# Feature-major products: three 256-column matmuls per k-tile into one range of PSUM, two feature blocks a bank

## The chip, the cores and the metric

The kernel runs on one core of one Trainium2 chip. The metric is the device time of one execution in microseconds; the median of several executions is compared. A core has a TensorE (PE, with its weight loads shown as PEld), a VectorE (DVE), a ScalarE (ACT), a GpSimd (POOL) and a SyncE (SP, which issues the DMAs here).

## What is computed

One decoder layer on 256 tokens of 2048 features, all in float32. Cut to what matters here:

```python
h = rms_norm(x, g_mix)
proj = h @ w_in                      # split into qkv_a, z_a, b_a, a_a, q_b, k_b, v_b, f_b, q_m, gates
qkv_a = causal_conv_silu(qkv_a, conv_w)     # 4 taps along the tokens, 3072 features
q_a, k_a, v_a = split(qkv_a)                # l2-normed, then the gated delta rule, 8 heads
...                                         # forgetting attention, memory attention, gated sum, w_out
x = x + y @ w_out
h2 = rms_norm(x, g_mlp)
x = x + square(relu(h2 @ w_ff1)) @ w_ff2    # 8192 hidden features

def causal_conv_silu(x, w):
    xp = pad(x, k_w - 1 zeros ahead of the first token)
    y = xp[:, 0:s] * w[0]
    for i in range(1, k_w):
        y = y + xp[:, i:i + s] * w[i]
    return silu(y)
```

## The kernel before

Every float32 product is made of three products of rounded parts: a matrix is split into a high part (rounded to the type fp32r) and a low part (the rest), and high x high, high x low and low x high are summed in PSUM. Weights come from HBM in chunks of 1 MB (`weights`, L155); each chunk is split in two halves by `split_half` (L146): an ACT copy rounds (L151), a DVE subtraction gives the rest (L152). Both are issued with a raised priority, so they run ahead of the products. There are 5 buffers for halves of either kind and 4 for chunks. Activations are split once, when they are made.

There are two kinds of product. `gemm_a` (L162) is token-major: an activation block of 128 x 128 is the stationary operand, a slice of 512 weight columns moves, and each k-tile (128 of the features that are summed over) has three matmuls of 512 columns for each of the two blocks of 128 tokens (L176 to L178). `gemm_b` (L191) is feature-major: a weight block of 128 x 128 is stationary and the 256 tokens move. It is called for pairs of feature blocks, 128 features each, with 16 k-tiles. It makes the q, k and v of the delta rule (`gdn_gemm`, L508, 24 blocks in 12 pairs) and the hidden layer of the squared-relu mlp (L925 on, 64 blocks in 32 pairs). Its activations stand as `Pairs` (L82): for each k-tile the 256 high and the 256 low columns are neighbours, so that `both(k)` is one operand of 512 columns. A k-tile then has two matmuls, both at L203: the high weights with the 512 columns into a whole bank of PSUM, and the low weights with the 256 high columns into its first half. In the last k-tile the two are issued in the opposite order. When a block is done, ACT copies the second half of the bank to SBUF (L205) and DVE adds the first half to it (L206) and writes the block's result to SBUF. For the convolution this result lies in a padded tile `xp` of 260 columns a block, whose first 4 are set to zero; ACT scales it by the first tap, DVE adds the other three (L500, L502). For the mlp ACT applies Relu (L931), DVE squares (L932), and `split` (L329) makes high and low parts.

The order of the work on each engine is the order of the program, raised priorities aside. Around the products run chains (the decay terms, the delta rule, attention) written as generators: `spawn` (L127) adds one, and `tick` (L131), called after each block and each chunk, runs one stage of every chain. `conv_pair` (L495) is such a chain: taps, then Silu and squares, then 8 one-column matmuls that sum the squares (L528), or transposes for v. PSUM is used as two pools of 4 banks, `pacc` for the products (tag `acc`) and one for all else (`sm`). One product stands apart: `head_scalars` (L402) has the three products of 256 columns each (L187 to L189, in `mm3`) with 96 weight columns.

Of the kernel before, what the change touches and what calls it, by code (L numbers as in the profile page):

```python
# [24 lines left out]
# columns of the packed vectors  # L25
# [3 lines left out]
# columns of the shape-only constants  # L29
# [10 lines left out]
def body(ctx: ExitStack, tc: tile.TileContext, I, out, dbg=None):  # L40
# [23 lines left out]
    class Blocks:  # L64
        """n blocks [128, 256], four to a tile"""
# [16 lines left out]
    class Pairs:  # L82
        """n blocks [hi 256 | lo 256], two to a tile"""
# [7 lines left out]

        def both(self, k):
            return self.t[k // 2][:, k % 2].rearrange("p a t -> p (a t)")
# [14 lines left out]
    # ---------------------------------------------------------------- constants  # L108
# [15 lines left out]
    # ---------------------------------------------------------------- interleaving  # L124
# [6 lines left out]
    def tick():  # L131
        """one more stage of each running chain"""
        for g in list(bg):
            if next(g, 0) == 0:
                bg.remove(g)
# [6 lines left out]
    # ---------------------------------------------------------------- weights  # L142
# [12 lines left out]
    def weights(src, ahead=PRI):  # L155
        """hi/lo of one chunk, in two halves"""
        with tc.high_priority(ahead):
            w = wtile(src.shape[1])
            nc.sync.dma_start(w, src)
            return [split_half(w, i) for i in range(2)]  # L160

    def gemm_a(srcs, act, evac, first=None, final=False):  # L162
        """token-major [2][128, 512] for one group of 512 columns"""
        ps = [acc(), acc()]
        nk = len(srcs) * 4
        for c, src in enumerate(srcs):
            parts = weights(src) if first is None else first[c]
            order = [(k4, tb) for k4 in range(4) for tb in range(2)]
            if final and c == len(srcs) - 1:
                order.sort(key=lambda o: o[1])  # L170
            for k4, tb in order:
                k = c * 4 + k4
                xh, xl = act(k)
                wh, wl = (t[:, k4 % 2 * 512:k4 % 2 * 512 + 512] for t in parts[k4 // 2])
                t = slice(tb * 128, tb * 128 + 128)
                mm(ps[tb], xh[:, t], wh, start=(k == 0), stop=False)  # L176
                mm(ps[tb], xh[:, t], wl, start=False, stop=False)  # L177
                mm(ps[tb], xl[:, t], wh, start=False, stop=(k == nk - 1))  # L178
                if final and k == nk - 1:
                    evac(tb, ps[tb])  # L180
            tick()
        for tb in range(2):
            if not final:
                evac(tb, ps[tb])
# [6 lines left out]
    def gemm_b(srcs, act, dst):  # L191
        """feature-major: chunks of [16 kt, 128 features], each into a [128, 256] of dst"""
        t = t2("lo")
        for f, src in enumerate(srcs):
            ps = acc()
            parts = weights(src)
            for k in range(KT):
                wh, wl = (t_[:, k % 8 * 128:k % 8 * 128 + 128] for t_ in parts[k // 8])
                ops = [(ps, wh, act.both(k)), (ps[:, 0:256], wl, act(k)[0])]
                if k == KT - 1:  # L200
                    ops.reverse()
                for i, (o, w, x) in enumerate(ops):
                    mm(o, w, x, start=(k == 0 and i == 0), stop=(k == KT - 1 and i == 1))  # L203
            tick()
            A.copy(t[:, f, :], ps[:, 256:512])  # L205
            V.tensor_tensor(dst[:, f, :], ps[:, 0:256], t[:, f, :], ALU.add)  # L206

    # ---------------------------------------------------------------- normed inputs
# [5 lines left out]
    def split_scaled(dst, xt, q, gcol, rows=None, ks=range(4)):  # L214
        """hi/lo of (transposed activations * gain [* a factor per token]) for 4 k-tiles"""
        for k in ks:
            g = pk[:, gcol + q * 4 + k:gcol + q * 4 + k + 1]
            h, l = dst(q * 4 + k)
            if rows is None:
                A.activation(h, xt[:, k, :], AF.Copy, scale=g)  # L220
                V.scalar_tensor_tensor(l, xt[:, k, :], g, h.bitcast(F32), ALU.mult, ALU.subtract)
            else:
                V.scalar_tensor_tensor(xt[:, k, :], xt[:, k, :], g, rows, ALU.mult, ALU.mult)
                A.copy(h, xt[:, k, :])
                V.tensor_tensor(l, xt[:, k, :], h.bitcast(F32), ALU.subtract)

    def row_stats(name, src):
        """1 / rms of each token"""
# [18 lines left out]
    # the first chunk and its k-tiles in halves, alternating  # L247
# [12 lines left out]
    def prep_x():  # L260
# [6 lines left out]
        # rstd of x along the free axis, on every partition  # L267
# [11 lines left out]
    # gains with the softmax scales folded in  # L279
# [4 lines left out]
    def head_scale(ps, rs, nh, dh, f2):  # L284
        """rstd of each head (times rs of the token)"""
# [15 lines left out]
    def heads_T(n, dst, tb, gains):  # L301
        """token-major [128, 512] transposed into dst[:, 0:4, tok block], gains per feature"""
# [18 lines left out]
    def query_T(ps, rs, nh, dh, dst, tb, gains, f2):  # L321
        """without the token's factor f2, which the logits get"""
        head_scale(ps, rs, nh, dh, f2)
        n = t2("hn", (P, 512))
        A.copy(n, ps)
        yield 1
        heads_T(n, dst, tb, gains)
# [5 lines left out]
    # ---------------------------------------------------------------- memory attention  # L333
# [60 lines left out]
    # ---------------------------------------------------------------- per-head scalars b, a, f  # L394
# [7 lines left out]
    def head_scalars():  # L402
# [15 lines left out]
        # log1p(e) = ln(u) + (e - (u - 1)) / u  # L418
# [5 lines left out]
        # rows 0..7: sigmoid(b) = exp(min(t, 0)) / u  # L424
        A.activation(beta, mn[0:32, :], AF.Exp)
        V.tensor_tensor(beta, beta, r_[0:32, :], ALU.mult)
        # rows 64..71: log f = min(t, 0) - log1p, and its running sum
# [3 lines left out]
        # rows 32..39: g = -exp(a_log) * softplus, running sums within chunks of 64  # L431
# [9 lines left out]
        # terms of j, per chunk of i  # L441
# [14 lines left out]
        # rows to every partition  # L456
# [3 lines left out]
        # columns: beta, cum, terms of j  # L460
# [11 lines left out]
    # E[j, i] = exp(decay from j to i), zero for j > i  # L472
# [17 lines left out]
    # ---------------------------------------------------------------- gated delta rule  # L490
# [4 lines left out]
    def conv_pair(xp, ft0, dst, then):  # L495
        """features ft0, ft0+1 of q/k/v: conv + silu -> dst [128, 2, 256]"""
        y = t2("cy")
        for f in range(2):
            cw = lambda i: pk[:, C_CONV + (ft0 + f) * 4 + i:C_CONV + (ft0 + f) * 4 + i + 1]
            A.activation(y[:, f, :], xp[:, f, 1:257], AF.Copy, scale=cw(0))  # L500
            for i in range(1, 4):
                V.scalar_tensor_tensor(y[:, f, :], xp[:, f, 1 + i:257 + i], cw(i), y[:, f, :], ALU.mult, ALU.add)  # L502
# [5 lines left out]
    def gdn_gemm(hf):  # L508
# [3 lines left out]
        # columns (k/q, token block, head): sums of squares  # L512
# [41 lines left out]
        for w, base in ((0, 8), (1, 0), (2, 16)):  # L554
            for pr_ in range(2):
                ft0 = base + hf * 4 + pr_ * 2
                xp = tp.tile([P, 2, 260], F32, tag="xp", name=nm("xp"), bufs=2)
                V.memset(xp[:, :, 0:4], 0.0)
                gemm_b([I["w_qkv"][ft0], I["w_qkv"][ft0 + 1]], hact, xp[:, :, 4:260])
# [5 lines left out]
                last = spawn(conv_pair(xp, ft0, dst, then))  # L565
# [4 lines left out]
    def gdn_chain(hf, st):  # L570
        kT, qT, vt, rq, sc = (st[n] for n in ("kT", "qT", "vt", "rq", "sc"))
        # M^T = KK * E * beta_j / |k_j|^2 ; A^T = QK * E * beta_j / |k_j|^2
        Eh = E[hf]
        # [0]: j in block 0, i in 0..255; [1]: j and i in block 1
# [15 lines left out]
        # (I + M) inverted for the 32x32 diagonal blocks, one per partition  # L590
# [5 lines left out]
        Mu = t4("Mu", (NU, 32, 32))       # [j, i]  # L596
        nc.sync.dma_start(Mu, dM.rearrange("t h (b j) i -> (t h b) j i", b=4))
        X = t4("X", (NU, 32, 32))         # [i, c]
# [40 lines left out]
        # transposed inverses of the 64x64 diagonal blocks  # L639
# [10 lines left out]
        # the solution, block by block, and the outputs  # L650
# [69 lines left out]
    # ---------------------------------------------------------------- forgetting attention  # L720
# [72 lines left out]
    # ---------------------------------------------------------------- gates and up projections  # L793
    y, yT = [], []

    def tok_tiles(name):
        """token-major [2][128, 2048] and its [128, 512] pieces"""
# [35 lines left out]
    # ---------------------------------------------------------------- the order of the parts  # L833
# [53 lines left out]
    # ---------------------------------------------------------------- output projection, residual  # L887
# [30 lines left out]
    # 1 / (mean(x^2) + eps), the square of rstd  # L918
# [6 lines left out]
    # ---------------------------------------------------------------- squared-relu mlp  # L925
    for q in range(4):
        u = Split("u", 16)
        for fp in range(8):
            r = t2("fr")
            gemm_b([I["w_ff1"][q * 16 + fp * 2 + i] for i in range(2)], h2, r)  # L930
            A.activation(r, r, AF.Relu)  # L931
            V.tensor_tensor(r, r, r, ALU.mult)  # L932
# [35 lines left out]
def prep(inp):  # L968
# [3 lines left out]
    def blk_a(w):        # [N/512, K/512, 128, 4*512]  # L972
# [4 lines left out]
    def blk_b(w):        # [N/128, 128, 16*128]  # L977
# [4 lines left out]
    def xT(x):           # [128, 16, 256]  # L982
# [52 lines left out]
```

## Time and profile before

| | |
|---|---|
| median of 3 runs | 1746.89 us (1746.37 to 1747.86) |
| span of the profiled execution | 1744.4 us |
| PE busy, matmuls | 1732.4 us, 8548 |
| PEld busy, weight loads | 1460.1 us, 8548 |
| DVE busy | 1037.3 us |
| ACT busy | 846.1 us |
| POOL busy | 40.5 us |
| read from HBM | 325.08 MB, 188 GB/s over the span |

The profile is of one execution; the median is of others, so the span stands beside it. Matmuls overlap each other: the time given for one reaches from its start to its end, and the next may start before. The distance of two starts is read from the timeline. A weight load overlaps with matmuls too.

### The profile page before, as it was taken

What the parts mean: (1) busy time and instruction counts of PE and PEld (TensorE: products, weight loads), DVE (VectorE), ACT (ScalarE), POOL (GpSimd) and SP (SyncE); (2) the same over time, 40 slices, a digit from 0 to 9 for tenths busy, and PEclk for the clock granted to TensorE, in tenths of its full rate; (3) what the DMA queues carried; (4) which work ended last, traced back from release to release, by engine and by line L of the source; (5) the groups of instructions that cost most, each with busy time, mean ns of one, the idle gap of its engine ahead of it and who ended that gap; (6) DMA issues with size and microseconds to landing.
All of it is one profiled execution on the core that took longest, in us unless ns stands there. A gap on an engine that the chain in (4) does not pass through costs nothing.

```text
span 1744.4 us, 21495 instructions
## 1 busy us (share of the span) xinstructions
PE 1732.4 (99%) x8548; PEld 1460.1 (84%) x8548; DVE 1037.3 (59%) x1379; ACT 846.1 (49%) x1144; POOL 40.5 (2%) x45
## 2 busy tenths in 40 slices
PE   8999999999999999999999999999999999999999
PEld 6888888888888888888888888888888888888887
DVE  5747777986654555555555566655665566556653
ACT  7656755435554345544444555533553355334542
POOL 0000000101000000000000000000000000000000
PEclk9999999999999999999999999999999999999999
DMA  9755444553545545455556555555555555555562
GB/s 380 286 190 173 145 166 151 174 173 132 183 142 193 193 170 204 172 193 193 190 198 233 176 190 190 181 194 192 184 193 193 193 186 177 195 196 187 193 200 90
DMA packets 53524, 329.11 MB, mean 189 GB/s; under 512 B 9888, under 2 KB 10544, under 8 KB 15664
## 3 DMA queue, kind: packets, MB, share of 16 engines
q1 hardware_dynamic: 53424, 327.74, 52.9%
q8 instruction: 67, 1.10, 0.2%
q14 instruction: 33, 0.27, 0.0%
HBM read 325.08 MB, written 2.64 MB: 188 GB/s over the span
## 4 chain that ended last, share of the span: by engine, by line
PE 99%; DVE 0%; DMA 0%; POOL 0%; ACT 0%; SPq 0%; issue 0%; DVEq 0%; POOLq 0%
PE acc L203 28%; PE acc L176 22%; PE acc L178 22%; PE acc L177 22%; PE sm L581 0%; PE sm L384 0%; PE sm L305 0%; PE sm L528 0%; PE sm L356 0%; DMA wf<-w_kv 0%; PE sm L670 0%; PE sm L664 0%; PE sm L899 0%; PE sm L785 0%; PE sm L688 0%; PE sm L675 0%
## 5 line engine op out<-in xcount | busy, mean ns | idle before, releaser
L152 DVE TENSOR_TENSOR wlo<-wf,whi 128x1024 fp32r<-128x1024 f32 x594 | 726.0, 1224 | 608.6 <-ACT whi L151 607.8
L151 ACT CAST whi<-wf 128x1024 fp32r<-128x1024 f32 x594 | 623.2, 1051 | 756.3 <-PE acc L178 556.6
L203 PE MATMUL acc<-h,whi 128*128 128x512 f32 x1408 | 496.0, 399 | 0.0
L203 PE MATMUL acc<-h,wlo 128*128 128x256 f32 x1408 | 380.8, 281 | 0.0
L203 PEld LDWEIGHTS acc<-h,whi 128*128 128x128 f32 x1408 | 260.2, 188 | 56.7
L176 PE MATMUL acc<-whi,h 128*128 128x512 f32 x704 | 278.2, 395 | 0.0
L178 PE MATMUL acc<-whi,h 128*128 128x512 f32 x704 | 274.4, 390 | 0.0
L177 PE MATMUL acc<-wlo,h 128*128 128x512 f32 x704 | 274.2, 389 | 0.0
L203 PEld LDWEIGHTS acc<-h,wlo 128*128 128x128 f32 x1408 | 265.8, 189 | 7.8
L176 PE MATMUL acc<-whi,uh 128*128 128x512 f32 x512 | 199.2, 389 | 0.0
L177 PE MATMUL acc<-wlo,uh 128*128 128x512 f32 x512 | 199.2, 389 | 0.0
L178 PE MATMUL acc<-whi,ul 128*128 128x512 f32 x512 | 199.2, 389 | 0.0
L178 PEld LDWEIGHTS acc<-whi,h 128*128 128x128 f32 x704 | 132.2, 188 | 28.1
L176 PEld LDWEIGHTS acc<-whi,h 128*128 128x128 f32 x704 | 132.2, 188 | 27.0 <-issue 0.5
L177 PEld LDWEIGHTS acc<-wlo,h 128*128 128x128 f32 x704 | 132.3, 188 | 26.4
L177 PEld LDWEIGHTS acc<-wlo,uh 128*128 128x128 f32 x512 | 96.1, 188 | 20.1
L178 PEld LDWEIGHTS acc<-whi,ul 128*128 128x128 f32 x512 | 96.1, 188 | 20.0
L176 PEld LDWEIGHTS acc<-whi,uh 128*128 128x128 f32 x512 | 96.1, 188 | 19.5
L176 PE MATMUL acc<-whi,mh 128*128 128x512 f32 x128 | 50.9, 400 | 7.4 <-ACT whi L151 7.4
L177 PE MATMUL acc<-wlo,mh 128*128 128x512 f32 x128 | 51.0, 398 | 0.0
L178 PE MATMUL acc<-whi,ml 128*128 128x512 f32 x128 | 50.8, 397 | 0.0
L176 PE MATMUL acc<-whi,yh 128*128 128x512 f32 x128 | 50.1, 392 | 0.0
(262 smaller groups left out, 1467.2 us busy)
## 6 DMA issues: line engine op xcount, KB each, us to landing
wf<-w_ff SPq DMA_DIRECT2D x128, 1024.0 KB, 4.7
wf<-w_gate SPq DMA_DIRECT2D x48, 1024.0 KB, 4.7
wf<-w_qkv SPq DMA_DIRECT2D x24, 1024.0 KB, 4.8
wf<-w_fox SPq DMA_DIRECT2D x24, 1024.0 KB, 4.8
wf<-w_up SPq DMA_DIRECT2D x24, 1024.0 KB, 4.8
wf<-w_out SPq DMA_DIRECT2D x16, 1024.0 KB, 4.8
wf<-w_kv SPq DMA_DIRECT2D x15, 1024.0 KB, 12.2
wf<-w_mq SPq DMA_DIRECT2D x8, 1024.0 KB, 4.8
```

Of the source, the lines that this page charges most:

```text
L151: A.copy(hi, c)
L152: V.tensor_tensor(lo, c, hi.bitcast(F32), ALU.subtract)
L176: mm(ps[tb], xh[:, t], wh, start=(k == 0), stop=False)
L177: mm(ps[tb], xh[:, t], wl, start=False, stop=False)
L178: mm(ps[tb], xl[:, t], wh, start=False, stop=(k == nk - 1))
L203: mm(o, w, x, start=(k == 0 and i == 0), stop=(k == KT - 1 and i == 1))
```

## The change

`gemm_b` takes one bank for a pair of feature blocks, 256 columns for each. A k-tile has three matmuls of 256 columns into the block's half: high weights with high columns, high weights with low columns, low weights with high columns. The sum of the three is formed in PSUM. Only the first matmul of a pair has the start flag and only the last the stop flag. The copy and the add behind each block are gone, and `gemm_b` returns the bank, seen as two blocks of 256. The convolution reads it directly: the last tap scales the block unshifted on ACT, and DVE adds the other three into the tokens from 1, 2 or 3 on, so that the padded tile, its zeroing and its buffers go. `gdn_gemm` runs the first stage of each convolution (the taps) at once with `next(last)`, not at the next tick. In the mlp Relu reads the bank, and the square is made by ACT in place of DVE. `both` is dropped; the layout of `Pairs` stays. Comments and docstrings are dropped as well; those lines are left out here.

```diff
@@ class Pairs
-        def both(self, k):
-            return self.t[k // 2][:, k % 2].rearrange("p a t -> p (a t)")
@@ gemm_b
-    def gemm_b(srcs, act, dst):
-        t = t2("lo")
+    def gemm_b(srcs, act):
+        ps = acc()
         for f, src in enumerate(srcs):
-            ps = acc()
+            o = ps[:, f * 256:f * 256 + 256]
             parts = weights(src)
             for k in range(KT):
                 wh, wl = (t_[:, k % 8 * 128:k % 8 * 128 + 128] for t_ in parts[k // 8])
-                ops = [(ps, wh, act.both(k)), (ps[:, 0:256], wl, act(k)[0])]
-                if k == KT - 1:
-                    ops.reverse()
-                for i, (o, w, x) in enumerate(ops):
-                    mm(o, w, x, start=(k == 0 and i == 0), stop=(k == KT - 1 and i == 1))
+                xh, xl = act(k)
+                mm(o, wh, xh, start=(f == 0 and k == 0), stop=False)
+                mm(o, wh, xl, start=False, stop=False)
+                mm(o, wl, xh, start=False, stop=(f == 1 and k == KT - 1))
             tick()
-            A.copy(t[:, f, :], ps[:, 256:512])
-            V.tensor_tensor(dst[:, f, :], ps[:, 0:256], t[:, f, :], ALU.add)
+        return ps.rearrange("p (f t) -> p f t", f=2)
@@ conv_pair
-    def conv_pair(xp, ft0, dst, then):
+    def conv_pair(ps, ft0, dst, then):
         y = t2("cy")
         for f in range(2):
             cw = lambda i: pk[:, C_CONV + (ft0 + f) * 4 + i:C_CONV + (ft0 + f) * 4 + i + 1]
-            A.activation(y[:, f, :], xp[:, f, 1:257], AF.Copy, scale=cw(0))
-            for i in range(1, 4):
-                V.scalar_tensor_tensor(y[:, f, :], xp[:, f, 1 + i:257 + i], cw(i), y[:, f, :], ALU.mult, ALU.add)
+            A.activation(y[:, f, :], ps[:, f, :], AF.Copy, scale=cw(3))
+            for i in (2, 1, 0):
+                n = 253 + i
+                V.scalar_tensor_tensor(y[:, f, 256 - n:], ps[:, f, 0:n], cw(i), y[:, f, 256 - n:], ALU.mult, ALU.add)
         yield 1
@@ gdn_gemm
-                xp = tp.tile([P, 2, 260], F32, tag="xp", name=nm("xp"), bufs=2)
-                V.memset(xp[:, :, 0:4], 0.0)
-                gemm_b([I["w_qkv"][ft0], I["w_qkv"][ft0 + 1]], hact, xp[:, :, 4:260])
+                ps = gemm_b([I["w_qkv"][ft0], I["w_qkv"][ft0 + 1]], hact)
...
-                last = spawn(conv_pair(xp, ft0, dst, then))
+                last = spawn(conv_pair(ps, ft0, dst, then))
+                next(last)
@@ squared-relu mlp
-            gemm_b([I["w_ff1"][q * 16 + fp * 2 + i] for i in range(2)], h2, r)
-            A.activation(r, r, AF.Relu)
-            V.tensor_tensor(r, r, r, ALU.mult)
+            ps = gemm_b([I["w_ff1"][q * 16 + fp * 2 + i] for i in range(2)], h2)
+            A.activation(r, ps, AF.Relu)
+            A.activation(r, r, AF.Square)
```

## Rows read from the trace of the kernel before

**Rows 1.** The page: busy time, granted clock in 40 slices, the chain by line.
```profile
PE 1732.4 (99%) x8548; PEld 1460.1 (84%) x8548; DVE 1037.3 (59%) x1379; ACT 846.1 (49%) x1144; POOL 40.5 (2%) x45
...
PEclk9999999999999999999999999999999999999999
...
PE acc L203 28%; PE acc L176 22%; PE acc L178 22%; PE acc L177 22%; PE sm L581 0%; PE sm L384 0%; PE sm L305 0%; PE sm L528 0%; PE sm L356 0%; DMA wf<-w_kv 0%; PE sm L670 0%; PE sm L664 0%; PE sm L899 0%; PE sm L785 0%; PE sm L688 0%; PE sm L675 0%
```

**Rows 2.** Waits of PE: what waited for what, us in total, times, longest.
```profile
PE acc L176 <- ACT whi L151: 7.4, 1, 7.4
PE sm L465 <- ACT Lm L365: 0.3, 1, 0.3
```

**Rows 3.** The page's groups: line, engine, operation, shapes, count | busy us, mean ns.
```profile
L203 PE MATMUL acc<-h,whi 128*128 128x512 f32 x1408 | 496.0, 399 | 0.0
L203 PE MATMUL acc<-h,wlo 128*128 128x256 f32 x1408 | 380.8, 281 | 0.0
...
L203 PEld LDWEIGHTS acc<-h,wlo 128*128 128x128 f32 x1408 | 265.8, 189 | 7.8
...
L176 PEld LDWEIGHTS acc<-whi,h 128*128 128x128 f32 x704 | 132.2, 188 | 27.0 <-issue 0.5
L177 PEld LDWEIGHTS acc<-wlo,h 128*128 128x128 f32 x704 | 132.3, 188 | 26.4
```

**Rows 4.** The chain in order of time, merged: start us, length us, what.
```profile
1207.85 90.45 PE acc L203 x512
```

**Rows 5.** Timeline of PE, end of a block: start us, length us, instruction, merged count.
```profile
1103.21 0.40 PE L203 MATMUL acc<-h,wlo 128*128 128x256 f32 x2
1103.45 0.63 PE L203 MATMUL acc<-h,whi 128*128 128x512 f32 x2
```

**Rows 6.** Timeline of PE in a stretch of `gemm_a`, 24 matmuls apart.
```profile
1300.18 0.39 PE L176 MATMUL acc<-whi,uh 128*128 128x512 f32 x1
...
1305.62 0.39 PE L176 MATMUL acc<-whi,uh 128*128 128x512 f32 x1
```

**Rows 7.** Timeline of PE in a quicker stretch of L203; first two rows 12 k-tiles apart.
```profile
292.49 0.39 PE L203 MATMUL acc<-h,whi 128*128 128x512 f32 x1
...
296.65 0.39 PE L203 MATMUL acc<-h,whi 128*128 128x512 f32 x1
...
297.23 0.40 PE L203 MATMUL acc<-h,wlo 128*128 128x256 f32 x2
297.46 0.40 PE L203 MATMUL acc<-h,whi 128*128 128x512 f32 x1
```

**Rows 8.** Timeline of PE: the first matmul of `head_scalars`, and the first after it.
```profile
144.17 0.28 PE L187 MATMUL sm<-h,whi 128*96 128x256 f32 x1
...
149.82 0.40 PE L203 MATMUL acc<-h,whi 128*128 128x512 f32 x1
```

**Rows 9.** Groups by form, 1035 to 1120 us, with idle time before and its releaser.
```profile
L152 DVE TENSOR_TENSOR wlo<-wf,whi 128x1024 fp32r<-128x1024 f32 x31 | 38.0, 1225 | 28.5 <-ACT whi L151 28.5
L151 ACT CAST whi<-wf 128x1024 fp32r<-128x1024 f32 x30 | 31.5, 1050 | 30.1 <-PE acc L203 30.1
L206 DVE TENSOR_TENSOR fr<-acc,lo 128x256 f32<-128x256 f32 x15 | 6.3, 418 | 0.0
L205 ACT COPY lo<-acc 128x256 f32<-128x256 f32 x15 | 5.4, 363 | 0.0
...
L932 DVE TENSOR_TENSOR fr<-fr 128x512 f32<-128x512 f32 x7 | 4.8, 685 | 0.0
L931 ACT ACTIVATE fr<-fr 128x512 f32<-128x512 f32 x7 | 4.4, 627 | 0.0
```

**Rows 10.** Groups by form, 150 to 316 us, the stage of q, k and v.
```profile
L502 DVE SCALAR_TENSOR_TENSOR cy<-xp,pk,cy 128x256 f32<-128x256 f32 x64 | 28.2, 482 | 2.9 <-ACT cy L500 2.7
L500 ACT ACTIVATE cy<-xp,pk 128x256 f32<-128x256 f32 x22 | 10.6, 508 | 0.8 <-DVE xp L206 0.8
...
L504 ACT ACT_TABLE_LOAD x4 | 5.1, 1283 | 0.1
```

## The prediction

> **What bounds the kernel now.** I read the page first. PE is busy for 1732.4 of 1744.4 us, and of the chain that ended last the two matmuls of `gemm_b` (L203) are 28% and the three of `gemm_a` (L176 to L178) 66% [rows 1]. A busy TensorE may still be one that is fed late, so I read the waits of PE next: two rows, 7.4 us at the very start and 0.3 us, and nothing at L203 [rows 2]. The granted clock is at the upper level, 2.4 GHz, in all 40 slices; DVE is busy for 59%, ACT for 49% [rows 1]. So the time is the number of matmuls times the spacing at which TensorE starts them, and every other engine works in its shadow. The change can move the end in one way of weight: by what one k-tile costs TensorE. The groups of L203 count 1408 k-tiles (88 blocks of 16), each with one 512-column and one 256-column matmul and a weight load for each [rows 3]. The means in these groups (399 and 281 ns) are latencies that overlap; for the cost I need start-to-start times, which the chain and the timeline give.
>
> **What a k-tile costs before.** In the squared-relu stage the chain has three runs of 90.45 us with 512 matmuls each, one of which is shown: 256 k-tiles, 353.3 ns a k-tile [rows 4]. That is 1408 x 353.3 = 497 us, the 28% of the page.
>
> **What it will cost after.** The k-tile becomes three 256-column matmuls, each with its own load of 128 weight columns. The moved columns are the same (768); a matmul and a load are added, 1408 of each. The trace has no long stream of 256-column matmuls with 128-column weights, so I bound the price from its neighbours.
>
> First, two 256-column matmuls in a row stand at the end of each block, where the last k-tile is reversed. In the steady squared-relu stage they start at 1103.21 and the 512 behind them 0.24 us later, as at the end of the next two blocks: 120 ns each [rows 5]. Second, by subtraction: the 512-column matmuls of `gemm_a` go at 24 in 5.44 us, 226.7 ns [rows 6]; in a quicker stretch of L203 twelve k-tiles take 4.16 us, 346.7 ns [rows 7]; 346.7 - 226.7 = 120 ns for the 256. Two roads give 120 ns, so three give **360 ns, 6.7 ns above the 353.3 of now**. The sum is 1408 x 6.7 ns = 9.4 us.
>
> Both ends of the unknown. Low: at the end of the quicker stretch the two in a row take only 0.23 us, 115 ns each [rows 7], so 345 ns, 1408 x -8.3 = -11.7 us. Exactly three 256-column matmuls per k-tile stand in the trace once, in `head_scalars` (L187 to L189), but with 96 weight columns: 16 k-tiles from 144.17 to 149.82, 353 ns, no difference [rows 8]. High: L203 mostly runs in the slower of two paces, 353.3 and not 346.7, 6.7 ns more over two matmuls; if each of the three pays that, 3 x (120 + 3.3) = 370 ns, +23.5 us; if the 256-column one had borne all of it, 3 x 126.7 = 380 ns, +37.5 us. I take 360: its two rows have the weight width and the moving size of the changed kernel, and `head_scalars` loads a quarter less per matmul.
>
> The Trainium skill, "TensorE: Matmul & The Clock Gate", section "Wait — 56ns, not 53.3ns?", gives a warm matmul of N columns N / 2.4 GHz and a fixed 2.5 ns or so. By it a 512 takes 215.8 ns, and the added matmul would cost 2.5 ns per k-tile, 3.5 us in all. That would put the time at 1750.4 us, the edge of no change, beside rival (a) below. The trace disagrees with the size: it shows 226.7 ns for that 512 [rows 6].
>
> **The evictions.** All of this lies beside TensorE. Removed, once in each of the 88 blocks: an ACT copy of 363 ns and a DVE add of 418 ns [rows 9], so 32 us of ACT and 37 us of DVE. Moved: 32 squares of 685 ns leave DVE (22 us) and become ACT squares; the nearest row is Relu of that shape, 627 ns, so 20 us [rows 9]. Should the square need another function table than Relu and the copies, a load of 1283 ns, as at L504 [rows 10], could come twice per pair, 2.6 us; bounds 0 and 2.6 us. Even then ACT has, per pair of blocks (32 x 353 ns = 11.3 us), 4 casts of 1050 ns, Relu, square and cast at some 0.63 us each and 2.6 us: 8.7 us. I cost it at nothing; the cover is that casts of the weights already wait for PE to free buffers, 30.1 us in 85 us [rows 9], so they run ahead. Without that cover each pair would pay its excess over 11.3 us.
>
> The convolution reads PSUM: 2 scaled copies on ACT (508 ns each now) and 6 taps on DVE (482 ns each) per pair [rows 10]. The zero padding of `xp` and its memsets go. I take the same durations; the nearest DVE row of that size that reads PSUM, the add L206, takes 418 ns with two tensor operands [rows 9], so the taps lie between 418 and 482. Its first stage moves: `next(last)` issues these 2 + 6 instructions straight behind the pair's matmuls, not after the next pair's first block, past the other chains' stages and weight splits of that block in the ACT and DVE queues; no DMA, SP or POOL instruction moves with it. Silu, the squares and their 8 small matmuls (L528) follow one tick earlier each. The wait of the first copy for the pair's last matmul holds up the ACT queue where L205 did so before, for the same matmul; the taps do it for DVE as L206 did. The small matmuls still come two blocks, 11.3 us, behind the taps, whose chain is 2 x 508 + 6 x 482 + two ACT passes of the size of Relu, 2 x 627, or 5.2 us. So nothing is late on TensorE.
>
> A bank is held by a pair until its last read, some 4 us beyond the last matmul. Before a pair took two banks of `pacc`, now one; of four, the same bank comes up three pairs later, 33.9 us. Nothing waits.
>
> **The rivals.**
> (a) *Cost goes by moved columns alone*, so that 768 columns cost the same in two matmuls or three, or nearly so. For it: `head_scalars` and L203 both take 353 ns [rows 4, 8]. Against it: L203 itself has two paces for the same columns [rows 4, 7], and `gemm_a` moves 512 columns in less than 512/768 of either [rows 6]. Time: no change, 1746.9 us.
> (b) *The slower pace for all three matmuls*, 370 ns: +23.5 us, 1770.4 us. For it: most of the L203 runs are in it [rows 4]. It decides if the stream locks into it from the first block on.
> (c) *The other side, faster*: a stream of equal matmuls runs as the pairs at 115 ns: -11.7 us, 1735.2 us. The mechanism is that in an even stream each load hides behind the matmul ahead of it without the loss that the uneven pairs show. It pays from 117.7 ns a matmul downwards. For it, the 0.23 us [rows 7]; against it, 0.24 us in the steady stage [rows 5].
> (d) *The change does not do what it says*: the same `wh` stands in two matmuls in a row, and its second load is left out; then the third matmul comes cheaper, at most back to the quick pace, 346.7 ns: -9.4 us, 1737.5 us. Against it: `gemm_a` uses `xh` twice in a row and has 704 loads for L176 and 704 for L177 [rows 3].
> (e) *TensorE waits for an eviction or a weight split* because an in-order queue is held: about 1 us at each of 44 pairs would give 44 us, 1791 us. It decides only if a pair's work on ACT or DVE passes 11.3 us; on DVE it is 4 x 1.22 + 6 x 0.48 = 7.8 us [rows 9, 10].
>
> **How the numbers follow.** The profiled execution has a span of 1744.4 us, 2.5 us under the median of 1746.89; I add the difference to the median. Forecast: 1746.9 + 9.4 = 1756.3 us (span 1753.8). Chances: forecast (356 to 364 ns) 0.46, (a) 0.24, (b) 0.18, (c) 0.07, (d) 0.02, (e) 0.03. The range takes in the forecast, (a) and (b), 0.88 of the chance, and no more of the low end than 351 ns, three times 117: 1744 to 1770.5 us. A measurement of this kernel tells some 0.2% from no change, 3.5 us or 2.5 ns a k-tile. Faster by more: (c), (d) and a little of (a), 0.10. Within: (a) and the low edge of the forecast, 0.25. Slower: the rest, 0.65.
>
> **What would show it.** The group of the `gemm_b` matmuls must have 4224 entries, all 128x256, and as many loads. Its long chain runs in the squared-relu stage should have 768 matmuls in 92.2 us for 256 k-tiles; 90.4 us speaks for (a), 94.7 us for (b), under 90 us for (c) or (d). PE's waits should stay under 10 us, L205 and L206 be gone, and DVE's busy time fall by some 60 us. I am wrong if the pace of `gemm_a` moves too, if PE waits appear at `gemm_b`, or if the stream of 256-column matmuls settles at another spacing than the two in a row did.

## The result, and the profile after

| | before | after |
|---|---|---|
| median of 4 runs each, us (range) | 1746.63 (1745.84 to 1747.86) | 1757.4 (1757.27 to 1757.6) |
| ratio to before, 95% interval | | 1.0061 (1.0047 to 1.0076) |
| span of the profiled execution, us | 1744.4 | 1755.4 |
| matmuls and weight loads, each | 8548 | 9956 |

The forecast was 1756.3 us, slower by 9.4; the kernel became slower by 10.8 us, the span by 11.0. The page after, answering to [rows 1]: busy time, the clock, the chain by line.

```profile
PE 1742.5 (99%) x9956; PEld 1535.5 (87%) x9956; DVE 994.7 (57%) x1247; ACT 843.9 (48%) x1088; POOL 40.1 (2%) x45
...
PEclk9999999999999999999999999999999999999999
...
PE acc L173 21%; PE acc L174 21%; PE acc L175 21%; PE acc L197 9%; PE acc L198 9%; PE acc L199 9%; DMA wf<-w_kv 1%; PE sm L576 0%; PE sm L379 0%; PE sm L300 0%; DVE wlo L149 0%; PE sm L351 0%; PE sm L524 0%; PE sm L665 0%; PE sm L659 0%
```

PE is still the chain, and its clock still at the upper level, 2.4 GHz. The waits of PE, answering to [rows 2]:

```profile
PE acc L173 <- ACT whi L148: 7.5, 1, 7.5
PE sm L543 <- ACT vT L500: 0.5, 1, 0.5
PE sm L370 <- ACT qTm L304: 0.3, 1, 0.3
PE acc L174 <- DVE wlo L149: 0.3, 1, 0.3
```

None is at the new matmuls (L197 to L199), and of the 11.0 us by which the span grew 10.1 are busy time of PE (1732.4 to 1742.5), so the 11 us are not waiting. The groups of these, answering to [rows 3], and their timeline in the steady squared-relu stage, two rows 13 k-tiles apart:

```profile
L197 PE MATMUL acc<-h,whi 128*128 128x256 f32 x1408 | 400.2, 284 | 0.0
L199 PE MATMUL acc<-h,wlo 128*128 128x256 f32 x1408 | 398.5, 283 | 0.0
L198 PE MATMUL acc<-h,whi 128*128 128x256 f32 x1408 | 398.4, 283 | 0.0
...
L198 PEld LDWEIGHTS acc<-h,whi 128*128 128x128 f32 x1408 | 270.2, 192 | 0.3
```

```profile
1216.03 0.28 PE L197 MATMUL acc<-h,whi 128*128 128x256 f32 x1
...
1220.71 0.28 PE L197 MATMUL acc<-h,whi 128*128 128x256 f32 x1
```

4.68 us for 13 k-tiles are 360 ns, 120 ns a matmul, the value of [rows 5]. Next, the stretches of `gemm_b` in both traces, each from its first matmul to the first of the next product (both ends are set one matmul, some 0.23 us, early): q, k and v, then the four quarters of the mlp. Columns: stretch, its length, busy time and instructions of PE, PEld, DVE, ACT and POOL, clock, DMA. Before:

```profile
149.59:315.91 166.32, 165.83 (x971) 145.51 (x970) 128.49 (x264) 103.11 (x166) 14.05 (x10) 1.00 0.46 160
1028.96:1120.40 91.44, 91.44 (x521) 79.27 (x520) 57.13 (x75) 48.44 (x73) 0.00 (x0) 1.00 0.52 184
1207.45:1297.90 90.45, 90.45 (x513) 78.46 (x512) 54.64 (x64) 45.01 (x61) 0.00 (x0) 1.00 0.52 186
1384.94:1475.39 90.45, 90.45 (x513) 78.46 (x512) 54.65 (x64) 45.01 (x61) 0.00 (x0) 1.00 0.53 186
1562.44:1652.88 90.44, 90.44 (x513) 78.45 (x512) 54.64 (x64) 45.01 (x61) 0.00 (x0) 1.00 0.53 186
```

After:

```profile
149.56:319.99 170.43, 169.68 (x1356) 166.64 (x1354) 131.97 (x247) 96.22 (x143) 16.25 (x12) 1.00 0.43 152
1032.82:1126.21 93.39, 93.39 (x777) 93.10 (x776) 47.88 (x53) 49.08 (x65) 0.00 (x0) 1.00 0.52 181
1213.28:1305.43 92.15, 92.15 (x769) 92.10 (x768) 45.40 (x42) 45.78 (x53) 0.00 (x0) 1.00 0.52 183
1392.50:1484.65 92.15, 92.15 (x769) 92.10 (x768) 45.40 (x42) 45.78 (x53) 0.00 (x0) 1.00 0.53 183
1571.72:1663.87 92.15, 92.15 (x769) 92.10 (x768) 45.40 (x42) 45.78 (x53) 0.00 (x0) 1.00 0.52 183
```

The five stretches are longer by 4.11, 1.95, 1.70, 1.70 and 1.71 us, 11.2 in all; nothing is left for the rest of the program. In the mlp DVE has 9 us less to do in each quarter and the time rises all the same. And the weight loads, busy for 87% of a quarter before, are busy for all of it after.

### The profile page after: what moved, and what is told of

It reads as the page before. It is cut to its first block, busy times and chain, and to the rows that moved or that the text cites. A ratio compares the mean times of both kernels' runs of the same rounds, so it can differ in the third digit from the quotient of the medians.

```text
span 1755.4 us, 24060 instructions
## 1 busy us (share of the span) xinstructions
PE 1742.5 (99%) x9956; PEld 1535.5 (87%) x9956; DVE 994.7 (57%) x1247; ACT 843.9 (48%) x1088; POOL 40.1 (2%) x45
## 4 chain that ended last, share of the span: by engine, by line
PE 96%; issue 1%; DVE 1%; DMA 1%; ACT 0%; POOL 0%; SPq 0%; DVEq 0%; ACTq 0%; POOLq 0%
PE acc L173 21%; PE acc L174 21%; PE acc L175 21%; PE acc L197 9%; PE acc L198 9%; PE acc L199 9%; DMA wf<-w_kv 1%; PE sm L576 0%; PE sm L379 0%; PE sm L300 0%; DVE wlo L149 0%; PE sm L351 0%; PE sm L524 0%; PE sm L665 0%; PE sm L659 0%
## 5 line engine op out<-in xcount | busy, mean ns | idle before, releaser
L197 PE MATMUL acc<-h,whi 128*128 128x256 f32 x1408 | 400.2, 284 | 0.0
L199 PE MATMUL acc<-h,wlo 128*128 128x256 f32 x1408 | 398.5, 283 | 0.0
L198 PE MATMUL acc<-h,whi 128*128 128x256 f32 x1408 | 398.4, 283 | 0.0
L198 PEld LDWEIGHTS acc<-h,whi 128*128 128x128 f32 x1408 | 270.2, 192 | 0.3
L197 PEld LDWEIGHTS acc<-h,whi 128*128 128x128 f32 x1408 | 270.1, 192 | 0.3
L199 PEld LDWEIGHTS acc<-h,wlo 128*128 128x128 f32 x1408 | 270.1, 192 | 0.0
```

The costliest lines, as they stand in the source:

```text
L197: mm(o, wh, xh, start=(f == 0 and k == 0), stop=False)
L198: mm(o, wh, xl, start=False, stop=False)
L199: mm(o, wl, xh, start=False, stop=(f == 1 and k == KT - 1))
```

## The experiments

Line numbers in the fences are those of each experiment's own code. The main measure is the spacing in the steady squared-relu stage, where nothing interrupts; the granted clock is at the upper level there in all runs. The runs with the matmuls alone, the alternating order and the groups of 8 are medians of 4, 7 and 10 executions; of each of the others there is one execution, so their totals are read beside the spacing only.

**The matmuls alone.** The kernel before, with the three matmuls of the change and all evictions as they were:

```diff
-                ops = [(ps, wh, act.both(k)), (ps[:, 0:256], wl, act(k)[0])]
...
+                xh, xl = act(k)
+                mm(ps[:, 0:256], wh, xh, start=(k == 0), stop=False)
+                mm(ps[:, 256:512], wh, xl, start=False, stop=False)
+                mm(ps[:, 0:256], wl, xh, start=False, stop=(k == KT - 1))
```

> The kernel before with the matmuls of the change alone: three of 256 columns per k-tile, high x high and low x high into the first half of the block's bank, high x low into the second. The copy, the add, the padded tile, the DVE square and one bank per block stay. Theory (each matmul of 256 columns costs TensorE 120 ns, evictions are hidden): the whole difference is there, 1757 to 1758 us, and a k-tile of the squared-relu stage takes 360 ns. Rival (part of the 11 us comes from the moved eviction work or from the bank being shared): less than that, towards 1750 us.

Measured: 1756.97 us, ratio 1.0058 (1.0041 to 1.0075). Its timeline, two rows 5 k-tiles apart, again gives 360 ns:

```profile
1213.62 0.28 PE L200 MATMUL acc<-h,whi 128*128 128x256 f32 x1
...
1215.42 0.28 PE L200 MATMUL acc<-h,whi 128*128 128x256 f32 x1
```

The split of the matmuls is the whole loss. The rest of the change (no copy, no add, one bank for two blocks, the square on ACT) is worth nothing that can be told: this kernel and the changed one differ by 0.4 us, and the kernel before alone moved by 1.5 us between its runs.

**What a matmul of 256 columns waits for: its moving or a load.** The changed kernel with one size cut at a time. First the third matmul moves 128 columns, then all three do in the 14 inner k-tiles of each block:

```diff
-                mm(o, wl, xh, start=False, stop=(f == 1 and k == KT - 1))
+                mm(o[:, 0:128], wl, xh[:, 0:128], start=False, stop=(f == 1 and k == KT - 1))
```

> The changed kernel with the third matmul (low weights) moving 128 columns and not 256; the low weights' part of the second 128 tokens is left out. From the two spacings 226.7 ns (512) and 120 ns (256) a matmul costs 13.3 ns and 0.4167 ns a column. Theory (cost is moved columns and a fixed part): the third takes 66.7 + ... = 53.3 + 13.3 = 66.7 ns, 53 ns less, 1408 x 53.3 ns = 75 us less, about 1682 us. Rival (120 ns is the time to load the next 128 weight columns): the third keeps 107 to 120 ns, 1739 to 1757 us.

```diff
+                n = 256 if k in (0, KT - 1) else 128
+                mm(o[:, 0:n], wh, xh[:, 0:n], start=(f == 0 and k == 0), stop=False)
...
+                mm(o[:, 0:n], wl, xh[:, 0:n], start=False, stop=(f == 1 and k == KT - 1))
```

> The changed kernel with all three matmuls of the 14 inner k-tiles moving 128 of the 256 tokens; those k-tiles' part of the other 128 tokens is left out. Theory (load floor): the spacing stays between 112 and 120 ns though half as much moves, 336 to 360 ns a k-tile, 1728 to 1757 us. Rival (cost is moved columns and 13.3 ns): 66.7 ns each, 1232 x 160 ns = 197 us less, about 1560 us.

Measured: 1757.19 us and 1784.49 us. In the first, a k-tile in the timeline (third matmul, then the next k-tile's three):

```profile
1224.29 0.22 PE L199 MATMUL acc<-h,wlo 128*128 128x128 f32 x1
1224.35 0.33 PE L197 MATMUL acc<-h,whi 128*128 128x256 f32 x1
1224.52 0.28 PE L198 MATMUL acc<-h,whi 128*128 128x256 f32 x1
1224.64 0.22 PE L199 MATMUL acc<-h,wlo 128*128 128x128 f32 x1
```

The short one is followed after 60 ns, but the next then takes 170 ns: from one third matmul to the next are 350 ns, against 360. In the second, two rows four inner k-tiles apart:

```profile
1259.77 0.28 PE L198 MATMUL acc<-h,whi 128*128 128x128 f32 x1
...
1261.11 0.28 PE L198 MATMUL acc<-h,whi 128*128 128x128 f32 x1
```

With half as much to move, a matmul still takes 1.34 us / 12 = 112 ns: that is what a load of 128 weight columns allows. It is no floor of a matmul as such, for the 60 ns above are shorter. And the kernel before shows the same number where almost nothing moves: its one-column matmuls at L528, each with a load of 128 columns, start 111 or 112 ns behind one another in 48 of 56 cases, and 26 to 31 ns in the rest. The price "13.3 ns and 0.4167 ns a column" is refuted: it wanted 66.7 ns for every matmul of 128 columns.

Neither total is read as a price, for in q, k and v the granted clock was not at its upper level throughout. A stretch of the first run and one of the second, the clock third from the end, as a mean over its two levels (1.2 and 2.4 GHz are 0.5 and 1.00):

```profile
170.00:330.00 160.00, 156.11 (x1229) 153.73 (x1229) 121.42 (x231) 82.78 (x117) 15.50 (x12) 0.96 0.42 149
169.00:205.00 36.00, 34.11 (x225) 32.86 (x224) 22.88 (x36) 20.96 (x32) 0.00 (x0) 0.78 0.38 141
```

TensorE had been less busy before the clock first fell: in the first run for 5.9 of the 8 us from 158 us on (7.6 in the changed kernel), in the second for 5.9 of the 9.3 us from 158 us on. In the first run the mlp gained 10.6 us by its spacing and q, k and v lost 10.0, so the total did not move.

**The other size: fewer weight columns.** The second matmul with 64 weight columns; then all three with 64, and with 32, in the 14 inner k-tiles:

```diff
-                mm(o, wh, xl, start=False, stop=False)
+                mm(o[0:64, :], wh[:, 0:64], xl, start=False, stop=False)
```

> The changed kernel with the second matmul (high x low) on 64 of the 128 weight columns; that part of the other 64 features is left out. Theory (the loads are hidden, a matmul costs by moved columns and a fixed part): all three spacings stay at 120 ns, 1757 us. Rival (the load sets the spacing): the matmul whose load has 64 columns starts earlier, its predecessor's spacing falls to the 107 ns or so that moving needs, 13 ns a k-tile, about 1739 us.

```diff
+                q = P if k in (0, KT - 1) else 64
+                mm(o[0:q], wh[:, 0:q], xh, start=(f == 0 and k == 0), stop=False)
...
+                mm(o[0:q], wl[:, 0:q], xh, start=False, stop=(f == 1 and k == KT - 1))
```

> The changed kernel with all three matmuls of the 14 inner k-tiles on 64 of the 128 weight columns; those k-tiles' part of the other 64 features is left out. Theory (a matmul's spacing is the longer of moving its own 256 columns and loading the next weights, the two nearly equal here; with short loads moving alone is left): about 117 ns each, as in head_scalars and in the run with one short load, 351 to 353 ns a k-tile, 1746 to 1748 us. Rival (every load takes its time on top, 8 ns a k-tile for each halved load as in that run): 336 ns a k-tile, 1232 x 24 ns = 30 us less, 1728 us.

> The changed kernel with all three matmuls of the 14 inner k-tiles on 32 of the 128 weight columns; those k-tiles' part of the other 96 features is left out. Theory C (price by loaded weight columns, 13.3 ns per 128, over 106.7 ns of moving): 106.7 + 3.3 = 110 ns each, 330 ns an inner k-tile, the steady 256 k-tiles of the squared-relu stage in 224 x 330 + 32 x 360 = 85.4 us. Theory S (256 columns need 113.3 ns by themselves, 226.7 for 512, and 128-column loads add the rest): no change against 64 columns, 340 ns, 87.8 us.

Measured: 1745.24, 1738.69 and 1742.99 us. The timelines: of the first, two rows 6 k-tiles apart; of the second, 5 k-tiles; of the third, 2 and, elsewhere, 7:

```profile
1211.77 0.28 PE L197 MATMUL acc<-h,whi 128*128 128x256 f32 x1
...
1213.87 0.28 PE L197 MATMUL acc<-h,whi 128*128 128x256 f32 x1
```

```profile
1210.91 0.28 PE L198 MATMUL acc<-h,whi 128*64 128x256 f32 x1
...
1212.61 0.28 PE L198 MATMUL acc<-h,whi 128*64 128x256 f32 x1
```

```profile
1239.91 0.28 PE L198 MATMUL acc<-h,whi 128*32 128x256 f32 x1
...
1240.59 0.28 PE L198 MATMUL acc<-h,whi 128*32 128x256 f32 x1
...
1220.40 0.28 PE L198 MATMUL acc<-h,whi 128*32 128x256 f32 x1
...
1222.87 0.28 PE L198 MATMUL acc<-h,whi 128*32 128x256 f32 x1
```

350 ns, then 340 ns, then 340 and 353 ns. Shortening one load of three gives half of the gain that is to be had, shortening all gives 113.3 ns a matmul, and shortening them further gives nothing more. Neither of my forecasts for 64 columns came (351 to 353 ns, or 336), and theory C, a price for every loaded column, is refuted (it wanted 330 ns with 32). What is left is the moving: 113.3 ns for 256 columns, half of the 226.7 ns of a 512 in `gemm_a` [rows 6]. The 353 ns shows that two paces exist with loads of 32 columns too: from the second quarter of the mlp on whole blocks take turns, 16 k-tiles at 353 and 16 at 341, and the mlp takes 5.5 us more than with 64.

**The same in the kernel before.** The 512-column matmul with 64 high weight columns, the 256-column one with 64 low ones, and both:

```diff
+                q = P if k in (0, KT - 1) else 64
-                ops = [(ps, wh, act.both(k)), (ps[:, 0:256], wl, act(k)[0])]
+                ops = [(ps[0:q], wh[:, 0:q], act.both(k)), (ps[:, 0:256], wl, act(k)[0])]          # high
+                ops = [(ps, wh, act.both(k)), (ps[0:q, 0:256], wl[:, 0:q], act(k)[0])]             # low
+                ops = [(ps[0:q], wh[:, 0:q], act.both(k)), (ps[0:q, 0:256], wl[:, 0:q], act(k)[0])]  # both
```

> The kernel before with the 512-column matmul of the 14 inner k-tiles on 64 of the 128 high weight columns; that part of the other 64 features is left out. Theory (the pair loses at the load that has only a 256-column matmul to hide behind, which is the high weights' load): that load is short now, the pair falls to 346.7 ns or below, 1232 x 6.7 ns = 8 us, 1738 us or less. Rival (the slower pace has another cause): 1746 to 1747 us.

> The kernel before with the 256-column matmul of the 14 inner k-tiles on 64 of the 128 low weight columns; that part of the other 64 features is left out. Theory (this load hides behind a 512-column matmul with 100 ns to spare): no change, 353.3 ns, 1746 to 1747 us. Rival (any load costs, wherever it stands): the pair falls by some 7 ns, 1738 us.

> The kernel before with both matmuls of the 14 inner k-tiles on 64 of the 128 weight columns; those k-tiles' part of the other 64 features is left out. Theory C (320 ns of moving and 6.7 ns for each half load): 333.3 ns an inner k-tile, the steady 256 k-tiles in 224 x 333.3 + 32 x 353.3 = 86.0 us. Theory S (768 columns need 340 ns by themselves): 340 ns, 87.5 us.

Measured: 1734.34, 1739.39 and 1733.28 us. The longest run of each in the chain, answering to [rows 4]; first high, then low, then both:

```profile
1203.90 87.65 PE acc L204 x512
```

```profile
1205.37 88.85 PE acc L204 x512
```

```profile
1202.77 87.66 PE acc L204 x512
```

With the two whole k-tiles of each block at 353.3 ns, the inner ones take (87.65 - 32 x 0.3533) / 224 = 341 ns, 346 ns and 341 ns. Shortening the load of the high weights, which has only the 256-column matmul to hide behind, takes away all of the 12 ns; then the load of the low weights no longer matters (341 with both). But shortened alone it does gain 7 ns, against what I expected. Its 346 ns are the quicker pace of [rows 7]; whether a load behind a 512 costs something in the slower pace, or only helps to set the pace, these runs do not tell. They do settle a rival: fewer weight columns also mean that a matmul writes fewer of the 128 partitions of PSUM, and writing might be the cost. With the high weights alone at 64 columns the 256-column matmul still writes all of them, and the k-tile takes 341 ns as it does with both at 64.

**The order in the kernel before.** Every second k-tile reversed, so that equal sizes stand behind each other, or 8 of one kind in a row:

```diff
-                if k == KT - 1:
+                if k % 2 == 1:
                     ops.reverse()
```

> The kernel before with its two matmuls per k-tile, their order reversed in every odd k-tile, so that 256 stands behind 256 and 512 behind 512. Theory A (the slower pace of 353.3 ns comes from a 512 and a 256 taking turns): the pair falls to 346.7 ns, 1408 x 6.7 ns = 9.4 us, about 1737 us. Theory B (order does not matter, the pair loses 6.7 ns wherever the columns stand): no change, 1746 to 1748 us.

```diff
...
+            for j, (hi, lo) in enumerate(parts):
+                ks = range(j * 8, j * 8 + 8)
+                big = [(ps, w8(hi, k), act.both(k)) for k in ks]
+                small = [(ps[:, 0:256], w8(lo, k), act(k)[0]) for k in ks]
+                ops += big + small if j == 0 else small + big
...
```

> The kernel before with its matmuls grouped: in each half block 8 of 512 columns and 8 of 256, the kinds in the opposite order in the second half, so that a block has 3 runs of equal matmuls. Theory (a load behind a 256 is as long as the moving, and each change between the two kinds costs): 8 x 226.7 + 8 x 120 ns, 346.7 ns a k-tile, 9 us less than before, 1737 to 1739 us. Rival (no more to gain than by alternating): 350.5 ns, 1741 to 1742 us.

Measured: 1741.51 us, ratio 0.9970 (0.9959 to 0.9981), and 1742.36 us, ratio 0.9979 (0.9969 to 0.9988). Their runs in the chain:

```profile
1206.86 89.17 PE acc L203 x512
```

```profile
1207.90 89.07 PE acc L205 x512
```

That is 348.3 and 347.9 ns a k-tile: neither theory of the first run holds, nor the spacing that either theory of the second gave; the gain is real but stops at 5 ns of the hoped 6.7. The one-line reversal beats both kernels: it is 5.2 us under the kernel before and some 16 us under the changed one.

## Why the prediction was right

**The bound and the covers.** Right: the time changed at `gemm_b` alone, PE gained no wait there, and the evictions were worth nothing (the run with the matmuls alone).

**The price of 360 ns.** Right in size, and [rows 5] are the right rows: there a 128-column load must hide behind 256 moving columns, as all three do in the changed kernel. The second road, the subtraction, came to the same 120 ns by luck. It took the 512 of the quick stretch at the 226.7 ns of `gemm_a`, but in each of those twelve k-tiles the 256 starts 0.23 us behind the 512, and what is left of their 4.16 us is 117 ns for a 256. The first pair:

```profile
292.49 0.39 PE L203 MATMUL acc<-h,whi 128*128 128x512 f32 x1
292.72 0.28 PE L203 MATMUL acc<-h,wlo 128*128 128x256 f32 x1
```

And with the slower pace for a minuend the same subtraction gives 126.7 ns, the prediction's own upper end. The prediction did not say why the price is 120; the runs do, and two prices that I put on record later (a fixed part for each matmul, a part for each loaded column) fell. Three matmuls cost as little as two where the loads are short: 340 ns in the changed kernel, 341 ns in that of before. So the added matmul itself is free. What costs is its load: by itself a load of 128 columns allows 112 ns a matmul, the moving by itself takes 113.3, and together they take 120. That is 6.7 ns over the moving for each matmul, and three times that, 20 ns, over the 340. Why two that are nearly equal do not hide each other fully is not shown.

**The sum, 9.4 us.** 1.4 to 1.8 us too small, and the stretches tell where. In the mlp 1024 k-tiles at 6.7 ns are 6.8 us, and 7.1 came. For q, k and v 384 k-tiles should give 2.6 us, and 4.1 came: I took 353.3 ns for all of before, though [rows 7] themselves show before at its quicker pace there. The chain of before has blocks of 16 k-tiles of either kind in that stage:

```profile
173.24 5.66 PE acc L203 x32
180.62 5.54 PE acc L203 x32
```

By the starts in the trace 12 of its 24 blocks keep 347 ns from end to end and 11 keep 353 (one is interrupted), 350.1 ns in the mean, and after the change the mean is 359.6. A step of 9.5 ns over 384 k-tiles gives some 3.7 of the 4.1 us; the rest is open. The term of q, k and v was mis-sized.

**The rivals.** (a), cost by columns alone, is half true: in the runs with loads of 64 columns three matmuls cost what two do. Its row, `head_scalars` with 96 columns [rows 8], lies between: 353 ns are 117.7 a matmul, over the 113.3 of 64 columns and under the 120 of 128, so it did pay for its loads in part, and its likeness to the 353.3 of L203 was chance. At 128 columns (a) fails. (b), a slower pace for all three, did not come: the 13 k-tiles of the timeline take 360 ns, and the quarters of 92.15 us leave no room. (c), loads hidden without a loss, exists, at 340 ns, but with 64 weight columns. (d) did not happen: L198 repeats the weights of L197 and has its 1408 loads. (e) did not happen.

**The signs.** The run of 768 matmuls was put at 92.2 us and is 92.15. DVE's busy time was to fall by some 60 us; it fell by 42.6 (1037.3 to 994.7). The durations of all DVE instructions, added up in each trace, do fall by 59.5 us, but neighbours overlap, and busy time counts an overlap once. The squares that moved to ACT cost nothing on the path, and no load of a function table came with them (18 in either trace). The conv taps read PSUM at 473 ns, within the 418 to 482 given:

```profile
L498 DVE SCALAR_TENSOR_TENSOR cy<-acc,pk,cy 128x255 f32<-128x255 f32 (+2 forms) x72 | 34.1, 473 | 1.9 <-ACT cy L495 1.1
```

The rule of the Trainium skill ("TensorE: Matmul & The Clock Gate", section "Wait — 56ns, not 53.3ns?"), N / 2.4 GHz and 2.5 ns, would give 109.2 ns for 256 columns, an estimate from the page's figures. The traces disagree: no run held a pace under 113 ns at this size, with loads as short as 32 columns, and the measurement decides.

## What to carry to other kernels

Before splitting one wide matmul into narrow ones on a TensorE-bound kernel, compare what each narrow one moves with what the next one loads: here a 128-column load hid behind 512 moving columns in `gemm_a` (226.7 ns, twice 113.3) and no longer fully behind 256 (120 ns for 113.3). Price it from places of the trace where the same moving width and the same weight width already stand behind each other, and check at which pace the stretch that is replaced really runs. Work taken off engines that wait for TensorE anyway bought nothing: DVE was busy for 43 us less, and the time was the same as with the matmuls alone.

## What was not expected of the hardware

- The load of 128 weight columns sets a floor to a stream: matmuls of 128 columns came every 112 ns. A single short one among wide ones moved most of the wait to its successor (60 ns, then 170 ns), and the k-tile gained 10 ns.
- The same instructions run at two paces: 346.7 or 353.3 ns before, 340 or 353 ns with 32 weight columns, and in both a block of 16 k-tiles keeps its pace. Runs with shorter loads or another order of the matmuls had other paces; what sets the pace is open.
- The scaled copy of the convolution on ACT has a new wait in the changed kernel, for the taps on DVE, 21.7 us in 7 times; in [rows 10] it waited for 0.8 us, and not for the taps. Copy and taps now read the same bank of PSUM; whether that is the reason is not shown. TensorE's own waits stayed under 9 us:

```profile
ACT cy L495 <- DVE cy L498: 21.7, 7, 5.0
```
